# HGRN heads of a hybrid streaming step: triangle work on VectorE, one-bank PSUM tiles, and tail pieces placed next to the level scores

## The chip, the core and the metric

The kernel runs on one core of a Trainium2 chip (trn2). The core has TensorE (PE; its weight loads are listed apart as PEld), VectorE (DVE), ScalarE (ACT), GpSimd (POOL) and the queue of SyncE (SP) that starts DMAs. Each engine works through its own queue in order and waits for others on semaphores. The metric is the device time of one execution in microseconds (us). All times below are of the kernel before.

## The reference

One step of an encoder layer: an mLSTM branch and an HGRN2 branch over the same 544 steps (512 of a new stream, 32 of a running one), merged by sigmoid gates. The change touches the HGRN2 branch alone, 8 heads of width 128:

```python
lfh = jnp.log(lb + (1.0 - lb) * jax.nn.sigmoid(f_lin))
kh = (1.0 - lb) * jax.nn.sigmoid(-f_lin)
qh = jax.nn.silu(q_h)
...
def _hgrn_chunk(S, inp):                    # one 64-step chunk of one head
    q, k, v, lf = inp
    g = jnp.cumsum(lf, axis=2)
    dec = jnp.exp(jnp.where(causal, g[:, :, :, None, :] - g[:, :, None, :, :], -jnp.inf))
    a = jnp.einsum('bhtc,bhtsc,bhsc->bhts', q, dec, k)
    o = jnp.einsum('bhtc,bhce->bhte', q * jnp.exp(g), S) + jnp.einsum('bhts,bhse->bhte', a, v)
    g_last = g[:, :, -1:, :]
    S_new = jnp.exp(g_last[:, :, 0, :])[..., None] * S + jnp.einsum('bhsc,bhse->bhce', k * jnp.exp(g_last - g), v)
    return S_new, o
...
oh = _head_rmsnorm(oh, hnorm_g) * jax.nn.silu(g_h)
yb = oh @ w_brh
y = sigmoid(ga) * ya + sigmoid(gb) * yb
```

The kernel returns the layer's output, the new states of both branches and the last rows of the convolution.

## The kernel before

The kernel is one instruction stream per engine, with 544 steps laid out along the free dimension and 128 channels on the partitions. First come the norm, the input projections and the mLSTM branch (heads 0 to 3, until about 645 us), then the eight HGRN heads (645 to 943 us), then the output projections.

**Projections as background.** Class `Pump` holds a list of projection blocks. A block is 12 or 24 matmuls into the PSUM tiles `d` (line 526), over split weights: ScalarE rounds a weight piece to its high part (`high_piece`, line 133), VectorE subtracts to get the low part (`low_piece`, 138) and forms sums of pieces (484). `pump.to(n)` emits background work up to step n, `pump.run(chain(h))` interleaves it with a generator's work: each `yield k` there lets k steps (12 matmuls each in this stage) pass. So the order of all engines around the change is written out by hand, through `STEPS`, `PIECES`, `TRICKLE` and the `yield`s, and PE, ACT and DVE run exactly this order (`manual_schedule`).

**A head.** `chain(h)` (the two scans are covered by running half of the stream backwards, so that one matmul serves both) builds the score tile `at`: 128 partitions by two blocks of 128 columns, and 32 more for the running stream. Step 0 makes the same-step scores `pd` (lines 1596, 1597; VectorE copies them through the mask `dmask` into `at` and `diag`, 1599, 1600). Then come seven levels c = 1, 2, 4 ... 64. Each needs the keys and queries scaled by the decays of that level: PE makes `pl` (1608, 1616), VectorE multiplies keys and queries for the next level (1625), multiplies neighbouring decays (1630), copies the level's scores into `at` where the level mask allows it (1636), and ScalarE gathers the next level's keys into `km` (1576). The queries of a new head are first multiplied by their decays (line 1469). At the end GpSimd splits `at` into its two triangles `aa` (1646 twice, 1652 for the running stream) and adds `diag` (1653).

**A tail.** `tail(h)` is cut at its `yield`s into pieces that are emitted while the next head's chain runs; `PIECES` says at which point (twice the level, plus one behind its scores; the entry (1, k) is two heads later). The pieces: transposes of values and of keys (`ht`, 1676, 1677; copied out by ScalarE, 1678, 1679), state products `su` (1686, 1687), their accumulation on VectorE (1692, 1702), the output `ho` (1710 to 1714), squares on ScalarE (1725), the inverse root on VectorE (181 to 188, spread by `TRICKLE`), the scaling on ScalarE (1731), and `finish`: transposes `hoT` (1755, 1756) and the gated product (1759, 1760).

**PSUM.** Eight banks of 512 floats. Four hold the `d` tiles. The others are two tiles `paux` of two banks each, used in turn by `pd`, `pl`, `ht`, `su`, `ho`, `hoT`: a new one waits until the last but one is read out. GpSimd zeroes `at`, `kit` and `osb` for each head anew (1569, 1670, 1717).

## Time and profile before

| | |
|---|---|
| median of three runs | 1157.86 us (1157.77 to 1157.99) |
| profiled execution | 1158.48 us, span 1156.8 us |
| granted TensorE clock | 0.998 |
| steady head (state of heads 2 to 6) | 33.79 us from key transposes to key transposes |
| PE, DVE, ACT, POOL busy within it | 32.47, 31.87, 24.38, 4.75 us |

The span lies within the execution's time: 1.7 us are outside of it. The page counts an engine as busy while an instruction is in it; matmul records overlap, so a PE that is listed as busy can still lose time. Losses are better read from the starts of matmuls that follow each other. A row of the timeline gives start, duration, engine, line, operation, output and inputs, and in brackets the idle time before it with what ended it.

### The profile page before, as it was taken

To read this page: it belongs to the slowest core of one execution; us is meant where nothing else is said; L and a number is where in the kernel's file an instruction comes from. 1 tells how busy PE (TensorE), PEld (TensorE's weight loads), DVE (VectorE), ACT (ScalarE), POOL (GpSimd) and SP (SyncE) were. 2 spreads that over 40 slices of the span, in tenths; PEclk is the share of its full clock that TensorE was granted. 3 is DMA by queue.
4 is the path that set the end of the run, shared out by engine and by line. 5 is a ranking of instruction groups with operands and counts; after the bars stand their busy time and mean duration, and the time that the engine had idled before them with its cause. 6 is when DMAs were issued, how large, how long until landed. Compare 5 with 4: busy or idle time off the path is not lost.

```text
span 1156.8 us, 23858 instructions
## 1 busy us (share of the span) xinstructions
PE 1130.9 (98%) x8937; PEld 1113.0 (96%) x8937; DVE 920.1 (80%) x2030; ACT 697.0 (60%) x1517; POOL 147.2 (13%) x306
## 2 busy tenths in 40 slices
PE   9989999999999999999999999999999999999998
PEld 8989999999999999999999999999999999999998
DVE  6876989576896777976887889999999988654585
ACT  5676647655666556664655477777667767433462
POOL 5833000111010110101200011111111100000000
PEclk9999999999999999999999999999999999999999
DMA  6143214322264132552636222212222343234653
GB/s 216 56 136 97 83 56 149 122 87 103 78 212 153 38 138 83 172 194 67 229 107 223 66 81 65 80 54 72 80 69 77 102 159 110 96 114 137 223 194 114
DMA packets 77899, 135.78 MB, mean 117 GB/s; under 512 B 8788, under 2 KB 16340, under 8 KB 77784
## 3 DMA queue, kind: packets, MB, share of 16 engines
q1 hardware_dynamic: 77616, 134.21, 35.7%
q8 instruction: 70, 1.15, 0.4%
q14 instruction: 45, 0.37, 0.1%
q10 hardware_dynamic: 168, 0.06, 0.0%
HBM read 109.32 MB, written 24.91 MB: 116 GB/s over the span
## 4 chain that ended last, share of the span: by engine, by line
PE 77%; DVE 16%; ACT 4%; issue 2%; DMA 2%; SPq 0%; ACTq 0%; DVEq 0%
PE d L526 29%; PE ya L167 8%; PE pg L1829 4%; PE yb L167 4%; PE o L167 4%; PE k L167 4%; PE C L1000 4%; PE q L167 4%; PE nm L1174 2%; PE sc L960 2%; DVE ws L484 2%; DVE hkq L1625 1%; PE pl L1608 1%; PE d L409 1%; DVE cv L723 1%
## 5 line engine op out<-in xcount | busy, mean ns | idle before, releaser
L1576 ACT COPY km<-hkq 128x256 f32<-128x256 f32 x56 | 23.9, 427 | 47.9 <-DVE hkq L1625 30.1
L543 ACT COPY t<-d 128x272 f32<-128x272 f32 x126 | 47.3, 376 | 5.1 <-PE d L526 4.7
L1625 DVE TENSOR_TENSOR hkq<-hkq,hq 128x288 f32<-128x288 f32 (+1 forms) x96 | 41.0, 434 | 6.1 <-PE pl L1616 4.7
L1608 PE MATMUL pl<-hkq,km 128*128 128x128 f32 x224 | 37.9, 291 | 4.1 <-ACT kit L1679 3.3
L723 DVE SCALAR_TENSOR_TENSOR cv<-ub,vec,cv 128x547 f32<-128x547 f32 x48 | 40.3, 841 | 0.6
L1608 PEld LDWEIGHTS pl<-hkq,km 128*128 128x128 f32 x224 | 31.0, 189 | 5.2 <-ACT kit L1679 4.0
L1103 DVE SCALAR_TENSOR_TENSOR c<-c,wi,Cs 128x258 f32<-128x258 f32 x32 | 15.3, 478 | 23.7 <-PE Cs L1101 23.6
L1012 ACT COPY Co<-C 128x258 f32<-128x258 f32 x32 | 10.4, 377 | 30.8 <-PE C L1000 24.0
L1636 DVE COPY_PREDICATED at<-lmask,pl 128x288 f32<-128x288 uint8 (+1 forms) x56 | 26.4, 471 | 0.0
L1646 POOL TENSOR_TENSOR aa<-at,tri 128x256 f32<-128x256 f32 x16 | 17.6, 1126 | 67.2 <-DVE at L1636 67.2
L1242 DVE TENSOR_TENSOR y<-ya,y 128x272 f32<-128x272 f32 x48 | 18.8, 434 | 8.1 <-PE ya L167 7.0
L1185 ACT COPY y<-nm 128x516 f32<-128x516 f32 x16 | 9.5, 591 | 22.6 <-PE nm L1174 22.6
L911 DVE TENSOR_TENSOR kl<-kf,kh 128x512 fp32r<-128x512 f32 x16 | 11.0, 688 | 13.9 <-ACT kh L910 11.9
L1652 POOL TENSOR_TENSOR at<-at,tri 32x32 f32<-32x32 f32 x8 | 4.8, 597 | 135.1 <-DVE at L1636 135.1
L974 ACT CAST sh<-dm 128x512 fp32r<-128x512 f32 (+3 forms) x16 | 7.3, 459 | 20.3 <-DVE dm L968 20.3
L1000 PE MATMUL C<-vh,kwh 128*128 128x258 f32 x96 | 19.4, 283 | 0.0
L1000 PE MATMUL C<-vh,kwl 128*128 128x258 f32 x96 | 19.3, 283 | 0.0
L1000 PE MATMUL C<-vl,kwh 128*128 128x258 f32 x96 | 19.3, 283 | 0.0
L960 PE MATMUL sc<-q,kh 128*128 128x512 f32 (+3 forms) x80 | 18.6, 321 | 0.1
L1133 DVE BATCH_NORM_STATS2 bs<-y 128x6 f32<-128x512 f32 (+1 forms) x20 | 13.8, 689 | 6.1 <-ACT y L1185 5.9
L887 POOL COPY vsm<-vt 128x96 f32<-128x96 f32 x16 | 7.3, 465 | 86.7 <-ACT vt L554 43.7
L1803 DVE TENSOR_TENSOR gb<-yb,gb 128x272 f32<-128x272 f32 x16 | 6.3, 436 | 15.0 <-PE yb L167 15.0
(4528 smaller groups left out, 5095.0 us busy)
## 6 DMA issues: line engine op xcount, KB each, us to landing
ya_d<-y SPq DMA_DIRECT2D x32, 272.0 KB, 3.0
y<-ya_d SPq DMA_DIRECT2D x24, 272.0 KB, 3.3
c<-in_C SPq DMA_DIRECT2D x16, 258.0 KB, 3.7
out_Cp<-Co SPq DMA_DIRECT2D x16, 258.0 KB, 2.6
out_Cs<-c SPq DMA_DIRECT2D x16, 258.0 KB, 2.4
x<-in_xT SPq DMA_DIRECT2D x8, 272.5 KB, 4.7
ya<-ya_d SPq DMA_DIRECT2D x8, 272.0 KB, 4.3
h<-in_xT SPq DMA_DIRECT2D x8, 272.0 KB, 5.0
```

Of the source, the lines that this page charges most:

```text
L167: PE.matmul(both[b][:m, :TH], part(w, off + k * step, m, x), xx[:, half(b)], start=(k == 0 and j == 0), stop=(k == n - 1 and j == 2),)
L484: V.tensor_tensor(q[name], x, y, ALU.add)
L526: PE.matmul(ps, ww[:, c], xx, start=(start and k == 0 and j == 0), stop=end, skip_group_check=not start,)
L543: S.copy(t, ps)
L723: V.scalar_tensor_tensor(cv[:, :547], ub[:, j : j + 547], vcol(V_CW + 4 * ft + j), cv[:, :547], ALU.mult, ALU.add)
L960: PE.matmul(pn[:, 0, :n], ks[f][x][:, j * P : (j + 1) * P], qs[f][y][:, NS + j * P : T], start=(f == 0 and i == 0), stop=(f == KH - 1 and ...
L1000: PE.matmul(pn[g][:, :VH], kw[b][x][:, f * P : (f + 1) * P], vv[b][y][:, g * VH : (g + 1) * VH], start=(b == 0 and j == 0), stop=(b == NB ...
L1576: S.copy(km.rearrange("p (n j c) -> p n j c", j=2, c=c), view(kk, HB, ((2 * c, NA // (2 * c)), (c - HB, 2), (1, c))),)
L1608: PE.matmul(pn[:, 0, b * P : (b + 1) * P], km[:, b * P : (b + 1) * P], view(qq, b * P, ((2 * c, P // (2 * c)), (HB + c, 2), (1, c))), star ...
L1625: V.tensor_tensor(x, x, t, ALU.mult)
L1636: V.copy_predicated(at[:, :n], lmask[:, li, :n], pn[:, 0, :n])
L1829: PE.matmul(ps, part(w, k * P, P, x), xx[:, c], start=(k == 0 and j == 0), stop=(k == KD - 1 and j == 2))
```

## The change

It takes GpSimd out of the HGRN stage. The lower triangle is kept in `at` itself by a multiplication with `down` on VectorE; the other tile `aa` starts as the diagonal of the second `pd` tile (times the identity, on VectorE) and takes the upper triangle of `at` through the mask `up`. Both run seven steps into the next head (`APART`). ScalarE, not VectorE, now copies the first `pd` tile into `at`. `at`, `kit`, `osb` and `hv` become pairs of tiles that are zeroed once (`hv` set to one). The two two-bank tiles become four tiles of one bank, in a pool that exists for this stage only. `PIECES`, `TRICKLE` and the `yield`s move the tail's pieces to stand directly before or behind a level's scores; the query product's delay goes from 2 to 3 steps.

```diff
+APART = 7
+FDELAY = (1, 2, 3)
+QDELAY = 3
...
-PIECES = ((0, 0), (0, 2), (0, 4), (0, 5), (0, 6), (0, 9), (0, 13), (1, 4))
-TRICKLE = (2, 2, 2)
+PIECES = ((0, 1), (0, 4), (0, 6), (0, 6), (0, 7), (0, 8), (0, 13), (1, 5))
+TRICKLE = (1, 1, 2)
...
-    pa = ctx.enter_context(tc.tile_pool(name="pa", bufs=2, space=bass.MemoryType.PSUM))
+    psum = {}
+
+    def aux_pool(name, bufs):
+        if psum:
+            psum["stack"].close()
+        psum["stack"] = ExitStack()
+        psum["a"] = psum["stack"].enter_context(
+            tc.tile_pool(name=name, bufs=bufs, space=bass.MemoryType.PSUM, side="right", reuse_waits="tile")
+        )
+
+    aux_pool("pa", 2)
+    ctx.callback(lambda: psum["stack"].close())
...
-        return pa.tile([P, 2, 512], F32, tag="a", name=name)
+        return psum["a"].tile([P, 2, 512], F32, tag="a", name=name)
+
+    def pone(name):
+        return psum["a"].tile([P, 512], F32, tag="b", name=name)
...
-    tri = cp.tile([P, 2, P], F32, name="tri")
-    pick(tri[:, 0, :], ALU.is_ge, 0, 1, -1, 1.0, 0.0)
-    pick(tri[:, 1, :], ALU.is_gt, 0, -1, 1, 1.0, 0.0)
+    down = cp.tile([P, HB], F32, name="down")
+    for b in range(2):
+        pick(down[:, b * P : (b + 1) * P], ALU.is_ge, 0, 1, -1, 1.0, 0.0)
+    G.memset(down[:, 2 * P :], 0.0)
+    G.tensor_copy(down[:NS, 2 * P :], down[:NS, :NS])
     sxt = cp.tile([P, P], F32, name="sxt")
-    dmask = cp.tile([P, HB], U8, name="dmask")
+    up = cp.tile([P, 2 * P], U8, name="up")
...
-        G.memset(dmask, 0.0)
...
+        pick(sxt, ALU.is_gt, 0, -1, 1, 1.0, 0.0)
+        V.tensor_scalar(
+            up.rearrange("p (b t) -> p b t", b=2),
+            sxt.rearrange("p (o t) -> p o t", o=1).to_broadcast([P, 2, P]),
+            1.0,
+            None,
+            ALU.is_equal,
+        )
...
-            pump.defer(2, lambda: V.tensor_tensor(qq[:, :T], t[:, :T], tf[:, :T], ALU.mult))
+            pump.defer(QDELAY, lambda: V.tensor_tensor(qq[:, :T], t[:, :T], tf[:, :T], ALU.mult))
...
-    diag = small("diag", [P, 2, P], bufs=1, tag="ksm")
-    G.memset(diag, 0.0)
+    aux_pool("pb", 4)
+    ats = [tp.tile([P, NA + P], F32, tag="bc", name=f"at{i}") for i in range(2)]
+    aas = tp.tile([P, 2, 2, P], F32, tag="kws", name="aas", bufs=1)
+    kits = [small(f"kit{i}", [P, 2, P], tag="qw") for i in range(2)]
+    osbs = [small(f"osb{i}", [P, P], tag="osb") for i in range(2)]
+    hvs = [small(f"hv{i}", [P, 5], tag="hv") for i in range(2)]
+    for i in range(2):
+        G.memset(ats[i][:, NA:], 0.0)
+        G.memset(kits[i], 0.0)
+        G.memset(osbs[i], 0.0)
+        G.memset(hvs[i], 1.0)
...
-        at = tp.tile([P, NA + P], F32, tag="bc", name=f"at{h}")
-        G.memset(at, 0.0)
+        at = ats[h % 2]
...
-                yield STEPS[li] // 2
+                yield STEPS[li]
                 advance(h, 0)
-                yield STEPS[li] - STEPS[li] // 2
-                pn = paux(f"pd{h}")
+                pn = pone(f"pd{h}0"), pone(f"pd{h}1")
                 for j in range(2):
                     for b in range(2):
                         x = slice(j * HB + b * P, j * HB + (b + 1) * P)
-                        PE.matmul(pn[:, j, b * P : (b + 1) * P], kk[:, x], q0[:, x], start=True, stop=True)
-                PE.matmul(pn[:, 0, NA:HB], kk[:, wide], q0[:, csmp], start=True, stop=True)
-                with tc.high_priority():
-                    V.copy_predicated(at[:, :HB], dmask, pn[:, 0, :HB])
-                    V.copy_predicated(diag.rearrange("p b t -> p (b t)"), dmask[:, :NA], pn[:, 1, :NA])
+                        PE.matmul(pn[j][:, b * P : (b + 1) * P], kk[:, x], q0[:, x], start=True, stop=True)
+                PE.matmul(pn[0][:, NA:HB], kk[:, wide], q0[:, csmp], start=True, stop=True)
+                S.copy(at[:, :NA], pn[0][:, :NA])
+                S.copy(at[:NS, NA:HB], pn[0][:NS, NA:HB])
+                aa = aas[:, h % 2]
+                V.tensor_tensor(
+                    aa,
+                    pn[1][:, :NA].rearrange("p (b t) -> p b t", b=2),
+                    ident.rearrange("p (o t) -> p o t", o=1).to_broadcast([P, 2, P]),
+                    ALU.mult,
+                )
             else:
-                yield STEPS[li] // 2
+                yield STEPS[li]
                 advance(h, 2 * li)
-                yield STEPS[li] - STEPS[li] // 2
-
-            pn = paux(f"pl{h}{c}")
+
+            pn = pone(f"pl{h}{c}")
             for b in range(2):
                 PE.matmul(
-                    pn[:, 0, b * P : (b + 1) * P],
+                    pn[:, b * P : (b + 1) * P],
                     km[:, b * P : (b + 1) * P],
                     view(qq, b * P, ((2 * c, P // (2 * c)), (HB + c, 2), (1, c))),
                     start=True,
                     stop=True,
                 )
             if smp:
-                PE.matmul(pn[:, 0, NA:HB], kk[:, wide], qq[:, csmp], start=True, stop=True)
+                PE.matmul(pn[:, NA:HB], kk[:, wide], qq[:, csmp], start=True, stop=True)
...
-                V.copy_predicated(at[:, :n], lmask[:, li, :n], pn[:, 0, :n])
+                V.copy_predicated(at[:, :n], lmask[:, li, :n], pn[:, :n])
...
-        aa = tp.tile([P, 2, 2, P], F32, tag="kws", name=f"aa{h}", bufs=1)
-        for j in range(2):
-            G.tensor_tensor(
-                aa[:, j],
-                at[:, :NA].rearrange("p (b t) -> p b t", b=2),
-                tri[:, j : j + 1, :].to_broadcast([P, 2, P]),
-                ALU.mult,
-            )
-        G.tensor_tensor(at[:NS, NA:HB], at[:NS, NA:HB], tri[:NS, 0, :NS], ALU.mult)
-        G.tensor_tensor(aa[:, 1], aa[:, 1], diag, ALU.add)
+        def apart():
+            V.copy_predicated(aa.rearrange("p b t -> p (b t)"), up, at[:, :NA])
+            V.tensor_tensor(at[:, :HB], at[:, :HB], down, ALU.mult)
+
+        pump.defer(APART, apart)
         hs[h].update(at=at, aa=aa, told=told, tsmp=tsmp)
...
-        kit = small("kit", [P, 2, P], tag="qw")
-        kts, its = kit[:, 0], kit[:, 1]
-        G.memset(kit, 0.0)
+        kts, its = kits[h % 2][:, 0], kits[h % 2][:, 1]
+        ps = None
         s0 = small("s0", [P, P], tag="qf")
         nc.sync.dma_start(s0, a["S0"][h])
-        for n, src, dst, dss in ((0, ii, it, its), (1, kk, kt, kts)):
-            pt = paux(f"ht{h}")
+        for src, dst in ((ii, it), (kk, kt)):
+            pt = pone(f"ht{h}")
             for b, (c, _, _) in enumerate(chunks):
-                PE.transpose(pt[:, 0, b * P : (b + 1) * P], src[:, c], ident)
-            PE.transpose(pt[:NS, 1, :P], src[:, csmp], ident)
-            S.copy(dst, pt[:, 0, :])
-            S.copy(dss[:NS], pt[:NS, 1, :P])
+                PE.transpose(pt[:, b * P : (b + 1) * P], src[:, c], ident)
+            if src is ii:
+                ps = pone(f"hs{h}")
+                for n, x in ((1, ii), (0, kk)):
+                    PE.transpose(ps[:NS, n * P : (n + 1) * P], x[:, csmp], ident)
+            S.copy(dst, pt)
+            if src is ii:
+                S.copy(kits[h % 2][:NS], two(ps[:NS, : 2 * P]))
             yield 1
-
-        pu = paux(f"su{h}")
+        pu, pv = pone(f"su{h}"), pone(f"sv{h}")
         for b in range(NB):
             c = slice(b * P, (b + 1) * P)
-            PE.matmul(pu[:, 0, c], kt[:, c], it[:, c], start=True, stop=True)
-        PE.matmul(pu[:, 1, :P], kts, its, start=True, stop=True)
+            PE.matmul(pu[:, c], kt[:, c], it[:, c], start=True, stop=True)
+        PE.matmul(pv[:, :P], kts, its, start=True, stop=True)
         sb = tf
-        S.copy(sb[:, :P], pu[:, 0, :P])
+        S.copy(sb[:, :P], pu[:, :P])
         yield 1
         for b, ti in ((1, 0), (2, 2), (3, 3)):
...
-        po = paux(f"ho{h}")
+        po, pq = pone(f"ho{h}"), pone(f"hp{h}")
         for b, (c, i, j) in enumerate(chunks):
             d = slice(b * P, (b + 1) * P)
-            PE.matmul(po[:, 0, d], aa[:, j, i, :], it[:, d], start=True, stop=(b == 0))
+            PE.matmul(po[:, d], (aa if j else at[:, :NA].rearrange("p (b t) -> p b t", b=2))[:, i, :], it[:, d], start=True, stop=(b == 0))
             if b:
-                PE.matmul(po[:, 0, d], qq[:, c], sb[:, (b - 1) * P : b * P], start=False, stop=True)
-        PE.matmul(po[:, 1, :P], at[:, wide], its, start=True, stop=False)
-        PE.matmul(po[:, 1, :P], qq[:, wide], s0, start=False, stop=True)
+                PE.matmul(po[:, d], qq[:, c], sb[:, (b - 1) * P : b * P], start=False, stop=True)
+        PE.matmul(pq[:, :P], at[:, wide], its, start=True, stop=False)
+        PE.matmul(pq[:, :P], qq[:, wide], s0, start=False, stop=True)
         ov = slot(f"ov{h}")
-        osb = small("osb", [P, P])
-        G.memset(osb, 0.0)
-        S.copy(ov[:, :NP], po[:, 0, :])
-        S.copy(osb[:NS], po[:NS, 1, :P])
-        hv, hr = small("hv", [P, 5]), small("hr", [P, 5])
-        V.memset(hv, 1.0)
+        osb = osbs[h % 2]
+        S.copy(ov[:, :NP], po)
+        S.copy(osb[:NS], pq[:NS, :P])
+        hv, hr = hvs[h % 2], small("hr", [P, 5])
...
+    aux_pool("pc", 2)
```

Places where this moves instructions, taken from head 2's chain (a digit behind a name is the head; `pl24` is head 2, level 4; rows of `d`, weights and the repeats of `ho` are left out at the dots).

PE at the border of two heads, before (`ht1` are head 1's transposes, values then keys):

```order
L1676 MATMUL ht1_10025<-ident_102,hi1_9394 128x128 x4
L1677 MATMUL ht1_10025<-ident_102,hi1_9394 32x128
...
L1596 MATMUL pd2_10061<-hq2_9592,hkq2_9901 128x128 x4
L1597 MATMUL pd2_10061<-hq2_9592,hkq2_9901 128x32
L1608 MATMUL pl21_10069<-hkq2_9901,km21_10000 128x128 x2
L1616 MATMUL pl21_10069<-hkq2_9901 128x32
...
L1676 MATMUL ht1_10100<-ident_102,hkq1_9461 128x128 x4
L1677 MATMUL ht1_10100<-ident_102,hkq1_9461 32x128
```

and in the change:

```order
L1621 MATMUL pd20_10054<-hq2_9594,hkq2_9914 128x128 x2
L1621 MATMUL pd21_10055<-hq2_9594,hkq2_9914 128x128 x2
L1622 MATMUL pd20_10054<-hq2_9594,hkq2_9914 128x32
L1638 MATMUL pl21_10064<-hkq2_9914,km21_10007 128x128 x2
L1646 MATMUL pl21_10064<-hkq2_9914 128x32
L1700 MATMUL ht1_10078<-ident_102,hi1_9415 128x128 x4
L1704 MATMUL hs1_10083<-ident_102,hi1_9415 32x128
L1704 MATMUL hs1_10083<-ident_102,hkq1_9482 32x128
...
L1700 MATMUL ht1_10176<-ident_102,hkq1_9482 128x128 x4
L1638 MATMUL pl24_10182<-hkq2_9914,km24_10137 128x128 x2
```

The value transposes stood 12 projection matmuls ahead of `pd` and the key transposes 12 behind `pl21`; now the first stand right behind `pl21` and the second right before level 4. The first pair of `pd` products and the second are separate tiles.

PE around state products and output, before:

```order
L1686 MATMUL su1_10155<-hi1_9394,hkq1_9461 128x128 x4
L1687 MATMUL su1_10155<-kit_10021 128x128
L1755 MATMUL hoT0_10162<-anti_121,ov0_9777 128x128 x2
L1755 MATMUL hoT0_10162<-ident_102,ov0_9777 128x128 x2
L1756 MATMUL hoT0_10162<-anti_121,osb_9778 128x128
...
L1608 MATMUL pl24_10189<-hkq2_9901,km24_10135 128x128 x2
L1616 MATMUL pl24_10189<-hkq2_9901 128x32
...
L1710 MATMUL ho1_10232<-hi1_9394,aa1_9993 128x128 x2
L1713 MATMUL ho1_10232<-kit_10021,at1_9546 128x128
L1714 MATMUL ho1_10232<-s0_10023,hkq1_9461 128x128
...
L1608 MATMUL pl28_10270<-hkq2_9901,km28_10197 128x128 x2
```

and in the change:

```order
L1713 MATMUL su1_10245<-hi1_9415,hkq1_9482 128x128 x4
L1714 MATMUL sv1_10246<-kit1_8773 128x128
L1638 MATMUL pl28_10260<-hkq2_9914,km28_10190 128x128 x2
L1646 MATMUL pl28_10260<-hkq2_9914 128x32
L1737 MATMUL ho1_10272<-hi1_9415,at1_8770 128x128 x2
...
L1740 MATMUL hp1_10273<-kit1_8773,at1_8770 128x128
L1741 MATMUL hp1_10273<-s0_10076,hkq1_9482 128x128
```

`su` and `ho` of head 1 had `hoT`, 24 projection matmuls and level 4 between them; now only level 8 stands between them.

DVE behind level 4, before:

```order
L1636 COPY_PREDICATED at2_9998<-lmask_2933,pl24_10189 128x288
L1692 SCALAR_TENSOR_TENSOR tf1_9240<-tf1_9240,hq1_9239,su1_10155 128x128 x3
L1702 SCALAR_TENSOR_TENSOR sn_10205<-s0_10023,hq1_9239,su1_10155 128x128
L138 TENSOR_TENSOR ws151l_10208<-ws151_9967,ws151h_10175 128x512
L484 TENSOR_TENSOR ws175_10214<-wi67r0_9965,wi67r1_10037 128x512
L484 TENSOR_TENSOR ws275_10216<-ws175_10214,wi75r0_9963 128x512
L1721 MEMSET hv_10247 128x5
L550 TENSOR_TENSOR hq3_10047<-d511_10046,t151_10073 128x272
L138 TENSOR_TENSOR wa2251l_10252<-wi59r1_9819,wa2251h_10218 128x512
```

and in the change:

```order
L1666 COPY_PREDICATED at0_8769<-lmask_2935,pl24_10182 128x288
L1784 SCALAR_TENSOR_TENSOR ob0_10201<-hoT0_10194,vec_78,hg0_9131 128x512
L1785 SCALAR_TENSOR_TENSOR ob0_10201<-hoS0_10195,vec_78,hg0_9131 128x32
L155 TENSOR_TENSOR ws151l_10204<-ws151_9980,ws151h_10162 128x512
L503 TENSOR_TENSOR ws175_10210<-wi67r0_9978,wi67r1_10031 128x512
L503 TENSOR_TENSOR ws275_10212<-ws175_10210,wi75r0_9976 128x512
L569 TENSOR_TENSOR hq3_10040<-d511_10039,t151_10068 128x272
L155 TENSOR_TENSOR wa2251l_10229<-wi59r1_9831,wa2251h_10214 128x512
L1719 SCALAR_TENSOR_TENSOR tf1_9261<-tf1_9261,hq1_9260,su1_10245 128x128 x3
L1729 SCALAR_TENSOR_TENSOR sn_10257<-s0_10076,hq1_9260,sv1_10246 128x128
```

The state accumulation (1692, now 1719) stood directly behind level 4's copy; now the gated product and five projection instructions are ahead of it.

28 lines of the change are left out of this document (10 added, 18 removed).

## The prediction

> **What bounds the kernel now.** First the page's busy shares:
>
> ```profile
> PE 1130.9 (98%) x8937; PEld 1113.0 (96%) x8937; DVE 920.1 (80%) x2030; ACT 697.0 (60%) x1517; POOL 147.2 (13%) x306
> ```
>
> TensorE is occupied nearly throughout, so the total moves only if TensorE loses less time between matmuls or gets fewer. GpSimd's 147 us bound nothing by themselves. Next the table by stretches, one steady head (from its key transposes to the next head's) and the end of the stage; columns are stretch, length, then busy time and instruction count of PE, PEld, DVE, ACT and POOL, PE clock, DMA share and GB/s:
>
> ```profile
> 779.12:812.91 33.79, 32.47 (x259) 31.72 (x260) 31.87 (x83) 24.38 (x59) 4.75 (x7) 1.00 0.20 69
> 880.48:943.00 62.52, 62.48 (x507) 62.02 (x508) 58.40 (x140) 42.94 (x110) 4.06 (x5) 1.00 0.36 112
> ```
>
> The clock is full, DMA is light. VectorE has 1.9 us of slack in the 33.79 us of a head, so it can fall behind TensorE but hardly catch up; ScalarE has over 9. Third, TensorE's waits within the HGRN stage (us in total, times, longest):
>
> ```profile
> PE pl L1608 <- ACT kit L1679: 3.3, 6, 0.6
> PE pd L1596 <- DVE at L1636: 2.6, 6, 0.5
> PE ht L1676 <- DVE diag L1600: 1.7, 6, 0.3
> ```
>
> Each occurs six times, at the borders of heads 2 to 7, and each is for a PSUM tile of the ring of two to be read out. The listed lengths are too short, since matmul records overlap. So, fourth, one such border in TensorE's timeline, read by starts:
>
> ```profile
> 710.99 0.29 PE L526 MATMUL d<-xfh,ws174l 128*128 128x272 f32 x1
> 711.56 0.63 PE L1676 MATMUL ht<-ident,hkq 128*128 128x128 f32 x4 [0.29 <-DVE diag L1600]
> ...
> 712.05 0.38 PE L526 MATMUL d<-xfh,wa2274h 128*128 128x272 f32 x1
> 712.26 0.29 PE L526 MATMUL d<-xfl,wa2274h 128*128 128x272 f32 x1
> 712.39 0.29 PE L526 MATMUL d<-xfh,wa2274l 128*128 128x272 f32 x1
> ...
> 713.66 0.64 PE L1608 MATMUL pl<-hkq,km 128*128 128x128 f32 x4
> ...
> 714.28 0.37 PE L526 MATMUL d<-xfh,ws251h 128*128 128x272 f32 x1
> ...
> 721.11 0.28 PE L526 MATMUL d<-xh,wa1251l 128*128 128x272 f32 x1
> 721.44 0.68 PE L1710 MATMUL ho<-hi,aa 128*128 128x128 f32 x4
> ...
> 739.89 0.29 PE L526 MATMUL d<-xh,wa1152l 128*128 128x272 f32 x1
> 740.60 1.13 PE L1596 MATMUL pd<-hq,hkq 128*128 128x128 f32 x8 [0.42 <-DVE at L1636]
> 741.57 0.31 PE L1597 MATMUL pd<-hq,hkq 128*128 128x32 f32 x2
> 742.43 0.92 PE L1608 MATMUL pl<-hkq,km 128*128 128x128 f32 x4 [0.55 <-ACT kit L1679]
> ...
> 743.33 0.37 PE L526 MATMUL d<-xfh,ws175h 128*128 128x272 f32 x1
> ```
>
> Ordinary `d` matmuls start 0.13 us apart (712.26 to 712.39). Against that spacing TensorE loses 740.60 - 740.02 = 0.58 us before `pd`; after `pd` (whose 32-column end takes about 0.1 from 741.57) some 0.72 before `pl`; 0.28 in `pl` itself, which takes 0.90 to the next `d` where an unhindered one takes 714.28 - 713.66 = 0.62; 711.56 - 711.12 = 0.44 before the key transposes; and 721.44 - 721.24 = 0.20 before `ho`. That is 2.22 us per head. Without them a head takes 31.57 us.
>
> **What makes VectorE late at the border.** Fifth, GpSimd and VectorE there:
>
> ```profile
> 740.60 2.20 POOL L1646 TENSOR_TENSOR aa<-at,tri 128x256 f32<-128x256 f32 x2 [8.54 <-DVE at L1636]
> 742.88 1.06 POOL L1653 TENSOR_TENSOR aa<-aa,diag 128x256 f32<-128x256 f32 x1
> ```
>
> ```profile
> 740.35 0.68 DVE L138 TENSOR_TENSOR wa2275l<-wi67r,wa2275h 128x512 fp32r<-128x512 f32 x1
> 740.95 1.27 DVE L1469 TENSOR_TENSOR hkq<-hq,tf 128x544 f32<-128x544 f32 x1
> 742.14 1.21 DVE L138 TENSOR_TENSOR ws252l<-ws,ws252h 128x512 fp32r<-128x512 f32 x1
> 743.28 1.22 DVE L484 TENSOR_TENSOR ws<-ws,wi52r 128x512 f32<-128x512 f32 x1
> 744.42 0.47 DVE L1599 COPY_PREDICATED at<-dmask,pd 128x288 f32<-128x288 uint8 x1
> 744.78 0.43 DVE L1600 COPY_PREDICATED diag<-dmask,pd 128x256 f32<-128x256 uint8 x1
> ```
>
> While GpSimd works on `aa` (740.60 to 743.94), three VectorE instructions that read two SBUF tiles are long: 1.27, 1.21 and 1.22 us; the one ahead, of the same shape as the second and third, takes 0.68. For the 544-column one the whole kernel shows both lengths (count, then min/median/max ns):
>
> ```profile
> L1469 DVE TENSOR_TENSOR hkq<-hq,tf x8: 712/1266/1272, 619.3 to 876.1; 128x544 f32<-128x544 f32 x8
> ```
>
> So the loss is 0.56 + 0.53 + 0.54 = 1.63 us per head, and it falls just where the new head's query product (line 1469, needed by `pl`), and the `pd` copies (needed to free the tile for the key transposes) are waited for.
>
> [...]
>
> **The change, part by part.**
>
> *GpSimd removed.* VectorE gains 1.63 us per head. The zeroings it also did delayed nobody on the path; they vanish at no gain.
>
> *VectorE's added work.* Two instructions of 256 columns (identity times `pd`; masked copy of the upper triangle), each like the 0.43 of row 744.78, and a product of 288 columns, half of the pair at 729.99 below, 0.46: +1.32. Removed: the two copies at 744.42 and 744.78, 0.90, and a tiny memset. Net VectorE gain 1.2 us per head: 31.87 to about 30.7. All three lie inside VectorE's queue; the triangle pair stands ahead of the level-2 scaling, where VectorE is at its tightest, but `ho` wants its result some three levels later.
>
> *ScalarE's added work.* A copy of 256 and one of 32 columns, less one of the two `kit` copies. Prices, from the page's groups (busy, mean ns) and a timeline:
>
> ```profile
> L543 ACT COPY t<-d 128x272 f32<-128x272 f32 x126 | 47.3, 376 | 5.1 <-PE d L526 4.7
> ```
>
> ```profile
> 740.12 0.51 ACT L1576 COPY km<-hkq 128x256 f32<-128x256 f32 x1
> 740.54 0.62 ACT L133 CAST ws252h<-ws 128x512 fp32r<-128x512 f32 x1
> ...
> 742.12 0.25 ACT L1679 COPY kit<-ht 32x128 f32<-32x128 f32 x1
> ```
>
> At most 0.38 + 0.25, less 0.25: +0.4 us on 24.4, hidden in ScalarE's waits for VectorE. But its place counts: the tile for the 32-row transposes (`hs`) is the fifth of a ring of four, so it waits until ScalarE has emptied `pd`. ScalarE was busy without a break from 740.12 to the end of `kit` at 742.37. Now the copies end after one more weight cast (0.5) and one `d` copy (0.3), less the `ht` and `kit` copies (0.7) and plus 0.6 of their own: about 743.1. With `pl` ending near 742.4 and the value transposes 0.5 behind it, `hs` comes at 742.9: a wait of 0 to 0.3. I take 0, because `pl` is held by something later, next.
>
> *PSUM ring of four.* `pd` now takes a tile that was emptied a level or more before: 0.58 goes. The key transposes move to level 4: 0.44 goes. What is late next is `pl`, through the query product in VectorE's queue. From the scaling after level 16 to that product VectorE runs without a pause:
>
> ```profile
> 728.76 0.61 PE L1608 MATMUL pl<-hkq,km 128*128 128x128 f32 x4
> ```
>
> ```profile
> 729.99 0.91 DVE L1625 TENSOR_TENSOR hkq<-hkq,hq 128x288 f32<-128x288 f32 x2
> ```
>
> that is 740.95 - 729.99 = 10.96 us, and the same instructions stand there afterwards. TensorE's way from the end of level 16 (728.76 + 0.62 = 729.38) to `pd` was 10.64 without the 0.58; the value transposes leave it (0.49, row 711.56 to 712.05 for the same size, and a re-entry of 0.08, below), and `pd` adds 1.1: 11.2 to `pl`. VectorE needs 0.1 to start, 10.96, 0.71 for the product and 0.1 to signal: 11.9. So `pl` waits 0.7 if VectorE meets level 16 on time, and 1.2 if it is as late there as now (729.99 - 729.38 = 0.6). I take 0.7, because VectorE has 1.2 us less to do. The 0.28 inside `pl` and 0.2 before `ho` I leave. Residue 1.2 (bounds 0 and 1.7) of the 2.22.
>
> *Pieces next to scores.* The first `d` after a piece takes 0.21 (712.05 to 712.26), not 0.13: 0.08 each. By the order, a head has 11 such returns before and 7 now: 4 x 0.08 = 0.3 us saved. The 32-row transposes are the same work.
>
> *Outside the heads.* The masks made at the start and the later `up` cost GpSimd about as much as `tri` and `dmask` did. VectorE's mask instruction waits for GpSimd's selection on `sxt`; a weight subtraction and a convolution step stand between, and if that cover fails it is one wait of about a microsecond. On SP the state's output DMA now goes behind one more weight load: earlier loads, no one waits. `QDELAY` moves nothing on VectorE. All counted as 0.
>
> *Sum.* Per head 2.22 - 1.2 + 0.3 = 1.3 us (bounds 2.5 and 0.8). Six borders: 7.8. The border of heads 0 and 1, where ScalarE rather than GpSimd is late, and the last head's tail: 1 together (0.3 to 2). Total 9 us (bounds 5 and 17). The profiled execution of 1158.5 becomes 1149.5; it stood 0.6 above the median, so the time is **1149 us** (1141 to 1153).
>
> **The rivals.**
>
> *Slower: VectorE's state sums.* `su` and `ho` had 24 projection matmuls between them; now only level 8 (0.62) does. The sums between them were at:
>
> ```profile
> 717.71 0.75 DVE L1759 SCALAR_TENSOR_TENSOR ob<-hoT,vec,hg 128x512 f32<-128x512 f32 x1 [0.67 <-PE hoT L1756]
> ...
> 719.84 0.92 DVE L1625 TENSOR_TENSOR hkq<-hkq,hq 128x288 f32<-128x288 f32 x2 [0.18 <-PE pl L1616]
> ...
> 721.19 1.10 DVE L1692 SCALAR_TENSOR_TENSOR tf<-tf,hq,su 128x128 f32<-128x128 f32 x3
> ...
> 722.46 0.68 DVE L138 TENSOR_TENSOR ws151l<-ws,ws151h 128x512 fp32r<-128x512 f32 x1
> ...
> 724.75 0.68 DVE L138 TENSOR_TENSOR wa2251l<-wi59r,wa2251h 128x512 fp32r<-128x512 f32 x1
> ```
>
> They came directly behind level 4. Now `ob` (0.75, and a small one) and the stretch from 722.46 to 725.35 (2.9) stand ahead, 3.7 us. From the end of level 4 VectorE needs 1.35 (719.84 to 721.19), 3.7 and 0.35 for the first sum, 5.4. TensorE reaches the `ho` that reads it after `hoT` (0.5), 24 projections (3.1), `su` (1.1), level 8 (0.6) and about 0.9 of `ho`: 6.2. So 0.8 us of slack decides. At the border VectorE reaches the `pd` copy 2.7 us after `pd` (744.42 against 741.7); were it 3.5 late at level 4, TensorE would lose 2.7 in each of seven heads, 19 us against the 9 saved: 1168. Against it: row 719.84 finds VectorE waiting for `pl`, so the lateness is worked off by then, and the 1.6 us are gone. Chance 0.10.
>
> *The waits change places.* `hs` waits for ScalarE (0.3 to 1 us), `pl` the full 1.2, `ho` a little: 0.3 to 0.8 us saved per head, 1153 to 1157. For it: ScalarE does not pause from 740.12 to 742.37, and the copies stand at the end of a longer run. Chance 0.16.
>
> *It doesn't do what it says.* The long instructions could come from something other than GpSimd, ScalarE's copies for instance. Then VectorE gets 0.4 us more per head, `pl` waits about 2 and the ring and the returns save some 0.5: 1155. Against it: the row with 0.71 and 1.27 for one form, and GpSimd's times beside it. Chance 0.04.
>
> *All of it goes.* If VectorE stays ahead, `pl` does not wait: 17 us, 1141. Chance 0.05.
>
> **How the numbers follow.** The forecast, 1141 to 1153, has the remaining 0.65. The range is 1141 to 1156: below the upper end lie the forecast and most of the second and third rival. A difference under 0.2%, 2.3 us, cannot be told from none. Faster: the forecast, the last rival and most of the second and third, 0.84; no change, 0.06; slower, 0.10.
>
> **What would show it.** The 544-column product must be 0.71 us in all heads and the two behind it about 0.68; GpSimd idle from 645 us. TensorE's waits for `at` before `pd` and for `diag` must be gone; `pl` at a border should wait for VectorE's query product, about 0.7. Steady heads should take 32.3 to 32.6 us. `ho` must not wait on line 1719, nor `hs` on line 1623; if either does by more than a microsecond per head, the forecast is wrong.

## The result: 1157.92 us before, 1149.84 us after

Medians of four executions each: 1157.92 us (1157.77 to 1158.10) before, 1149.84 us (1148.69 to 1151.14) after; ratio 0.993, 95% interval 0.9913 to 0.9948. Forecast: 1149, with 1141 to 1156 as the range. The profiled execution of the changed kernel took 1151.14 us, its span is 1148.7.

The page's busy shares of the changed kernel, then one steady head in the table by stretches (stretch, length, busy time and count of PE, PEld, DVE, ACT, POOL, PE clock, DMA share, GB/s):

```profile
PE 1127.3 (98%) x8937; PEld 1114.4 (97%) x8937; DVE 910.1 (79%) x2029; ACT 699.5 (61%) x1525; POOL 111.4 (10%) x260
```

```profile
773.67:805.98 32.31, 31.65 (x262) 31.54 (x261) 30.75 (x83) 24.55 (x61) 0.00 (x0) 1.00 0.24 76
```

A head now takes 32.31 us from key transposes to key transposes, against 33.79. VectorE has 30.75 us of work in it (31.87 before), ScalarE 24.55 (24.38), GpSimd none. TensorE's waits from 640 to 975 us of the changed kernel:

```profile
PE pl L1638 <- DVE hkq L1487: 4.6, 7, 0.7
```

Of the three waits of the kernel before, those ahead of `pd` and of the transposes are gone, and the one ahead of `pl` has changed its releaser. One border in TensorE's timeline of the changed kernel:

```profile
738.42 0.29 PE L545 MATMUL d<-xh,wa1152l 128*128 128x272 f32 x1
738.55 1.11 PE L1621 MATMUL pd<-hq,hkq 128*128 128x128 f32 x8
739.49 0.31 PE L1622 MATMUL pd<-hq,hkq 128*128 128x32 f32 x2
740.46 0.89 PE L1638 MATMUL pl<-hkq,km 128*128 128x128 f32 x4 [0.66 <-DVE hkq L1487]
741.18 0.31 PE L1646 MATMUL pl<-hkq 128*128 128x32 f32 x2
741.33 0.64 PE L1700 MATMUL ht<-ident,hi 128*128 128x128 f32 x4
741.80 0.27 PE L1704 MATMUL hs<-ident,hi 128*32 128x128 f32 x1
```

`pd` follows `d` at the ordinary 0.13 us, `ht` and `hs` follow without a gap. By starts, `pl` comes 0.97 us behind the end part of `pd`, which needs 0.14 where nothing waits (646.85 to 646.99 in the first head), so 0.83 us are lost. On VectorE, what held it is the product of 739.59, behind a weight subtraction:

```profile
738.63 0.45 DVE L1666 COPY_PREDICATED at<-lmask,pl 128x256 f32<-128x256 uint8 x1
738.98 0.69 DVE L155 TENSOR_TENSOR wa2275l<-wi67r,wa2275h 128x512 fp32r<-128x512 f32 x1
739.59 0.72 DVE L1487 TENSOR_TENSOR hkq<-hq,tf 128x544 f32<-128x544 f32 x1
740.23 0.69 DVE L155 TENSOR_TENSOR ws252l<-ws,ws252h 128x512 fp32r<-128x512 f32 x1
740.83 0.68 DVE L503 TENSOR_TENSOR ws<-ws,wi52r 128x512 f32<-128x512 f32 x1
741.43 0.42 DVE L1626 TENSOR_TENSOR aas<-pd,ident 128x256 f32<-128x256 f32 x1
```

The instructions that took 1.27, 1.21 and 1.22 us take 0.72, 0.69 and 0.68. From the first `pd` to the first matmul of the stage that follows, the HGRN heads take 325.7 us (645.96 to 971.70) where they took 335.1 (645.03 to 980.14): 9.4 us less. The span became 8.1 us shorter; the rest was lost outside the heads, which comes at the end.

### The profile page after: what moved, and what is told of

It is laid out like the page before. It is cut to its first block, busy times and chain, and to the rows that moved or that the text cites. A ratio compares the mean times of both kernels' runs of the same rounds, so it can differ in the third digit from the quotient of the medians.

```text
span 1148.7 us, 23733 instructions
## 1 busy us (share of the span) xinstructions
PE 1127.3 (98%) x8937; PEld 1114.4 (97%) x8937; DVE 910.1 (79%) x2029; ACT 699.5 (61%) x1525; POOL 111.4 (10%) x260
## 4 chain that ended last, share of the span: by engine, by line
PE 80%; DVE 13%; ACT 3%; DMA 2%; issue 2%; SPq 0%; ACTq 0%; DVEq 0%
PE d L545 31%; PE ya L184 8%; PE yb L184 4%; PE pg L1855 4%; PE o L184 4%; PE k L184 4%; PE C L1019 4%; PE q L184 4%; PE nm L1193 2%; PE sc L979 2%; PE pl L1638 2%; PE d L428 2%; DVE hkq L1655 1%; DVE cv L742 1%; DVE ws L503 1%
## 5 line engine op out<-in xcount | busy, mean ns | idle before, releaser
L1842 DVE TENSOR_TENSOR h<-o,h 128x272 f32<-128x272 f32 x16 | 6.3, 436 | 15.0 <-PE o L184 13.2
L1193 PE MATMUL nm<-vh,sh 128*128 128x258 f32 x80 | 16.4, 287 | 0.1
L1193 PE MATMUL nm<-vl,sh 128*128 128x258 f32 x80 | 16.2, 284 | 0.0
```

The costliest lines, as they stand in the source:

```text
L1193: PE.matmul(pn[:, g, :VH], st[j][x][:, (i - j) * P : (i - j + 1) * P], vv[j][y][:, g * VH : (g + 1) * VH], start=(j == 0 and q == 0), stop ...
```

## The experiments

Twelve kernels were run, each beside the kernel before on the same chip. "Head" is the median interval between the starts of `pd` in the steady heads, read from TensorE's timeline of one profiled execution; outside a dip of the clock it repeats within 0.1 us from head to head (one head of e5, 0.35 us longer, excepted), and so tells more than the whole time, whose executions scatter by 1.3 us (e12) to 6 us (e5).

| Kernel | median us (range, executions) | before, same chip | ratio, 95% interval | head us |
|---|---|---|---|---|
| before | 1157.92 (1157.77 to 1158.10, 4) | | | 33.79 |
| changed | 1149.84 (1148.69 to 1151.14, 4) | 1157.92 | 0.993, 0.9913 to 0.9948 | 32.32 |
| e1 GpSimd load | 1150.36 (1149.71 to 1153.08, 6) | 1158.53 | 0.993, 0.9917 to 0.9943 | 32.31 |
| e2 two tiles of two banks | 1168.91 (1168.19 to 1169.58, 4) | 1158.53 | 1.0085, 1.0072 to 1.0098 | 34.77 |
| e3 old places | 1153.75 (1152.01 to 1154.22, 5) | 1158.53 | 0.995, 0.9938 to 0.9963 | 32.78 |
| e4 GpSimd's part alone | 1160.35 (1159.28 to 1163.00, 11) | 1158.53 | 1.0015, 1.0006 to 1.0024 | 33.82 |
| e5 GpSimd kept | 1163.76 (1161.90 to 1167.85, 6) | 1158.67 | 1.0041, 1.0026 to 1.0057 | 34.13 |
| e6 e4, old transposes | 1158.94 (1156.51 to 1160.76, 12) | 1158.67 | 1.000, 0.9991 to 1.0008 | 33.68 |
| e7 e3, old transposes | 1152.04 (1150.94 to 1152.52, 5) | 1158.67 | 0.9936, 0.9924 to 0.9948 | 32.88 |
| e8 product first | 1148.21 (1147.03 to 1150.24, 4) | 1158.67 | 0.9905, 0.9891 to 0.9919 | 32.19 |
| e9 GpSimd on the product | 1152.68 (1151.94 to 1155.37, 5) | 1158.36 | 0.9953, 0.9941 to 0.9965 | 32.58 |
| e10 sums later | 1153.21 (1152.54 to 1156.09, 6) | 1158.36 | 0.9956, 0.9944 to 0.9968 | 33.03 |
| e11 `hs` in `pd` | 1149.73 (1148.88 to 1151.08, 4) | 1158.36 | 0.9924, 0.9911 to 0.9937 | 32.40 |
| e12 with fillers | 1149.67 (1148.99 to 1150.27, 4) | 1158.36 | 0.9922, 0.9909 to 0.9935 | 32.40 |

### Is it GpSimd? (e1, e9)

```diff
+        G.tensor_copy(sxt[:, 0:2], at[:, 0:2])
+        for _ in range(6):
+            G.tensor_tensor(sxt, down[:, :P], ident, ALU.mult)
         pump.defer(APART, apart)
```

> The changed kernel, with GpSimd given six products of 128x128 (two SBUF inputs, result into a tile nobody reads) at the end of each head, where it made the triangles before; nothing else differs. Theory A (contention with GpSimd was the 1.63 us per head): the query product (line 1487) grows from 0.72 to about 1.25 us and the two or three VectorE instructions behind it grow too; TensorE's wait before `pl` grows from 0.66 to about 1.2 us; a steady head takes 32.9 to 33.9 us, the whole 1154 to 1160. Rival (the long instructions came from something else, which the change also removed): line 1487 stays at 0.72, the whole stays at 1149 to 1151.

Nothing moved: a head takes 32.31 us. GpSimd and VectorE at one border of this kernel:

```profile
737.36 0.51 POOL L1678 COPY sxt<-at 128x2 f32<-128x2 f32 x1 [27.23 <-DVE at L1666]
737.94 4.48 POOL L1680 TENSOR_TENSOR sxt<-down,ident 128x128 f32<-128x128 f32 x6
```

```profile
737.74 0.72 DVE L1487 TENSOR_TENSOR hkq<-hq,tf 128x544 f32<-128x544 f32 x1
738.37 0.94 DVE L155 TENSOR_TENSOR ws252l<-ws,ws252h 128x512 fp32r<-128x512 f32 x1
739.24 0.94 DVE L503 TENSOR_TENSOR ws<-ws,wi52r 128x512 f32<-128x512 f32 x1
```

The product had started 0.2 us ahead of the load and kept its 0.72; the two behind it grew to 0.94. So GpSimd does lengthen them, as theory A has it, but time lost behind the product costs TensorE nothing. e9 leaves the copy out, so that the load begins earlier, its first product reading `at`:

```diff
+        for j in range(6):
+            G.tensor_tensor(sxt, (down if j else at)[:, :P], ident, ALU.mult)
         pump.defer(APART, apart)
```

> The changed kernel with the same GpSimd load as in the first run (six products of 128x128 per head), begun some 0.6 us earlier, so that the query product runs under it. In the first run such a load lengthened a VectorE instruction with two SBUF inputs by 0.26 us (0.68 to 0.94), and nothing was lost because the product had already started. Theory A (contention costs time only through the query product, which `pl` waits for): the product takes about 0.98 us, the wait before `pl` grows from 0.66 to 0.9 us or a little more, a steady head from 32.32 to 32.6 (up to 32.8 if the subtraction ahead is hit as well), the whole about 1152. Rival (a load on GpSimd takes no time from TensorE here at all): 32.32 and 1150.

```profile
771.02 0.69 DVE L155 TENSOR_TENSOR wa2276l<-wi68r,wa2276h 128x512 fp32r<-128x512 f32 x1
771.63 0.98 DVE L1487 TENSOR_TENSOR hkq<-hq,tf 128x544 f32<-128x544 f32 x1
772.53 0.94 DVE L155 TENSOR_TENSOR ws253l<-ws,ws253h 128x512 fp32r<-128x512 f32 x1
```

The product grew by 0.26 us and the head by 0.26 (32.58): theory A, to the hundredth. Contention is real, and its price is what it adds to this one instruction.

### One part alone, and each part undone (e2 to e7)

e2 undoes the ring: two tiles of two banks, everything else as changed. What is shown for `pd` is done for the other pairs (`ht` and `hs`, `su` and `sv`, `ho` and `hp`, `hoT` and `hoS`) and for `pl`, which uses the first bank.

```diff
-    aux_pool("pb", 4)
+    aux_pool("pb", 2)
-                pn = pone(f"pd{h}0"), pone(f"pd{h}1")
+                pn = pone2(f"pd{h}")
+    def pone2(name):
+        t = paux(name)
+        return t[:, 0], t[:, 1]
```

> The changed kernel with its four one-bank PSUM tiles put back into two of two banks; GpSimd idle, pieces at the new places. Theory A (ring and places belong together): `ho` now needs the tile that `su` used, and the state sums leave that 1.3 us later than `ho` is reached; the key and value transposes need the tile of `pd`, read out 0.5 us too late; 1.5 to 2 us per head, so 1160 to 1165, slower than the kernel before. Rival (the ring is worth only the wait before `pd` and that before the transposes, and GpSimd the rest): 1152 to 1155.

TensorE's waits in this kernel's heads:

```profile
PE ho L1737 <- DVE sn L1729: 8.6, 7, 1.2
PE pl L1639 <- DVE hkq L1488: 4.6, 7, 0.7
PE ht L1701 <- DVE aas L1627: 4.2, 7, 0.6
```

The two waits that theory A named, 1.2 and 0.6 us, came, and the head lost more than that, 2.45 us: by starts they cost 1.40 and 0.79, and `hoT` comes 0.23 late as well. The whole, 1168.91, lies above the 1165 expected. The new places cannot be had without the ring.

e3 puts the places back, e4 places and ring, which leaves GpSimd's part (idle GpSimd, triangles on VectorE, `pd` read out by ScalarE). The step is split in the same way at the first level.

```diff
-PIECES = ((0, 1), (0, 4), (0, 6), (0, 6), (0, 7), (0, 8), (0, 13), (1, 5))
-TRICKLE = (1, 1, 2)
+PIECES = ((0, 0), (0, 2), (0, 4), (0, 5), (0, 6), (0, 9), (0, 13), (1, 4))
+TRICKLE = (2, 2, 2)
-                yield STEPS[li]
-                advance(h, 2 * li)
+                yield STEPS[li] // 2
+                advance(h, 2 * li)
+                yield STEPS[li] - STEPS[li] // 2
```

> The changed kernel with the head-tail's pieces back at the old places, in the middle of the steps (old PIECES, TRICKLE and split steps); ring of four and idle GpSimd stay. Theory A (places are worth the cheaper returns to `d`, 4 per head at 0.08): about 0.3 us per head, 1151 to 1153. Rival (the places also set when buffers come free or who is late, so they are worth a us per head or more): 1156 or more. A second rival: the old places are better, since they leave the state sums more time: 1147 or less.

> Only the first part of the change: triangles on VectorE and tiles zeroed once, with two two-bank PSUM tiles and the old places. Theory A (VectorE's 1.2 us per head pays even in the old ring): the wait before `pd` (0.58) goes and the one before the key transposes shrinks, the one before `pl` stays on ScalarE's copy; about 1 us per head, 1150 to 1153. Rival (without the ring the waits are for the tiles themselves and hardly move): 1155 to 1158.

Both were spoiled by something I had overlooked. The waits of e3:

```profile
PE hs L1706 <- DVE hkq L1657: 6.9, 7, 1.5
```

The changed tail makes both 32-row transposes in its first piece. At the old place that piece stands ahead of the new head's `pd`, where the old head's keys have not had their last scaling; e4 has the same wait. So both were run again with the transposes as in the kernel before, one behind each piece (`ps` is the second bank of the piece's tile in e6, a tile of its own in e7):

```diff
-            if src is ii:
-                ps = pone(f"hs{h}")
-                for n, x in ((1, ii), (0, kk)):
-                    PE.transpose(ps[:NS, n * P : (n + 1) * P], x[:, csmp], ident)
+            PE.transpose(ps[:NS, :P], src[:, csmp], ident)
```

> GpSimd's part alone once more: two two-bank PSUM tiles, old places, and now also the old order of the 32-row transposes (one behind each of the two pieces). The run with GpSimd's part alone that moved both 32-row transposes into the first piece took 1160.35, and TensorE waited there up to 1.5 us for the last scaling of the keys (line 1658). Theory A (that wait was the only thing that spoiled it, 6.9 us in all): 1152 to 1155. Rival (idle GpSimd is worth nothing in the old ring): 1157 to 1160.

> The changed kernel with the old places and the old order of the 32-row transposes; ring of four and idle GpSimd stay. With the old places alone it took 1153.75, 6.9 us of it waiting at `hs` for the keys' last scaling. Theory A (the wait at `hs` goes and nothing takes its place; what remains are 4 cheaper returns per head): 1147 to 1150, no worse than the changed kernel, so that the new places are worth nothing by themselves. Rival (the wait at `pl` for the query product, which `hs` had hidden, comes back with 4 to 5 us): 1151 to 1154.

e6, GpSimd's part alone, is worth nothing on balance: 1158.94 beside 1158.67, 0.11 us per head. Of the three waits of the kernel before, those ahead of `pl` and `pd` stay, the one ahead of the key transposes is gone, and one ahead of `hoT` is new:

```profile
PE pl L1641 <- ACT kit L1706: 4.1, 7, 0.6
PE pd L1623 <- DVE at L1669: 2.3, 6, 0.4
PE hoT L1779 <- DVE at L1669: 1.1, 6, 0.2
```

By starts the key transposes no longer lose their 0.44 us (they follow the `d` ahead of them by 0.13 instead of 0.57), and the stretch from `su` to `hoT` takes 0.36 longer (1.47 instead of 1.11): `hoT` needs a tile that VectorE reads out only behind its two new triangle instructions (0.86 us), which stand ahead of the level-2 scaling. So this part does free TensorE of one wait right behind the border, and the work that replaces GpSimd's costs nearly as much in the ring of two.

VectorE did get its 1.63 us back, 1.2 net of the added work, and spent most of that waiting. In its timeline of e6 one head has these waits:

```profile
775.67 0.42 DVE L1628 TENSOR_TENSOR aas<-pd,ident 128x256 f32<-128x256 f32 x1 [1.30 <-ACT at L1626]
...
782.96 0.75 DVE L1783 SCALAR_TENSOR_TENSOR ob<-hoT,vec,hg 128x512 f32<-128x512 f32 x1 [0.35 <-PE hoT L1780]
...
785.07 0.92 DVE L1658 TENSOR_TENSOR hkq<-hkq,hq 128x288 f32<-128x288 f32 x2 [0.18 <-PE pl L1649]
...
791.09 0.92 DVE L1658 TENSOR_TENSOR hkq<-hkq,hq 128x288 f32<-128x288 f32 x2 [0.43 <-PE pl L1649]
```

The kernel before has the last three of them too (0.66, 0.18 and 0.43), 1.27 us in all where e6 has 2.26. So the time that GpSimd took from VectorE behind one border had been made up some 10 us later, long before the next border, and giving it back moved nothing there: `pd` and `pl` lose 0.54 and 0.76 us by starts, where they lost 0.58 and 0.72. The 1.30 us is for ScalarE's copies out of the same two-bank tile; with one-bank tiles (e7) VectorE does not wait there.

e7 adds the ring: 1152.04, 0.80 us per head better than e6. The wait that remains, ahead of `pl`, is for ScalarE's copy of the value transposes (`hi`, 5.7 us in seven times). Theory A had expected no wait; the rival had the size, 4 to 5 us, but not the releaser. From e7 to the changed kernel, places and transposes together are worth 0.56 us per head.

e5 asks the reverse: ring and places as changed, GpSimd's part as before, with its zeroings and with `pd` read out by the two masked copies on VectorE.

```diff
-        pump.defer(APART, apart)
+        for j in range(2):
+            G.tensor_tensor(
+                aa[:, j],
+                at[:, :NA].rearrange("p (b t) -> p b t", b=2),
+                tri[:, j : j + 1, :].to_broadcast([P, 2, P]),
+                ALU.mult,
+            )
+        G.tensor_tensor(at[:NS, NA:HB], at[:NS, NA:HB], tri[:NS, 0, :NS], ALU.mult)
+        G.tensor_tensor(aa[:, 1], aa[:, 1], diag, ALU.add)
```

> The changed kernel's ring of four and its places, with the triangles, zeroings and masked `pd` copies of the kernel before, so that GpSimd works on `aa` at each border again. The first run of this series put a GpSimd load there, but it began after the query product had started, and the time did not move. Theory A (what costs time is that GpSimd hits the query product, which `pl` waits for): the product takes 1.2 to 1.3 us, TensorE waits 1.1 to 1.3 us before `pl` instead of 0.66, 0.5 us per head, 1153 to 1156. Theory B (VectorE as a whole is late by the 1.63 us and TensorE loses it all at the next levels): 1158 to 1162. Rival (GpSimd costs nothing once the ring and the places are new): 1149 to 1151.

At 1163.76 it is slower than the kernel before. One border, TensorE and then VectorE:

```profile
778.00 0.89 PE L1624 MATMUL pl<-hkq,km 128*128 128x128 f32 x4 [1.20 <-ACT ws476h L150]
...
780.59 0.28 PE L1697 MATMUL hs<-ident,hi 128*32 128x128 f32 x1 [1.08 <-DVE at L1616]
```

```profile
776.60 1.26 DVE L1486 TENSOR_TENSOR hkq<-hq,tf 128x544 f32<-128x544 f32 x1
777.78 1.23 DVE L155 TENSOR_TENSOR ws253l<-ws,ws253h 128x512 fp32r<-128x512 f32 x1
778.93 1.21 DVE L501 TENSOR_TENSOR ws<-ws,wi53r 128x512 f32<-128x512 f32 x1
780.07 0.46 DVE L1616 COPY_PREDICATED at<-dmask,pd 128x288 f32<-128x288 uint8 x1
```

The product ends at 777.86, 0.14 us ahead of `pl`, so that is what `pl` waits for, whatever the row names. That costs 0.54 us more than in the changed kernel, as theory A had it; the other 1.08 is `hs`, which needs a `pd` tile that VectorE empties behind three long instructions. The sum, 1.62, is most of the 1.81 us per head between the two kernels; by starts the two come to 0.53 and 1.24, 1.77. Theory B had about the size (1.63 us per head; the time lies above its 1162) and not the place.

These runs also show what sets how late VectorE is at level 16, from where it runs without a pause to the query product. Level 16 and VectorE's scaling behind it, in e5 with GpSimd at work, and in e6 with GpSimd idle:

```profile
799.05 0.61 PE L1624 MATMUL pl<-hkq,km 128*128 128x128 f32 x4
799.84 0.92 DVE L1641 TENSOR_TENSOR hkq<-hkq,hq 128x288 f32<-128x288 f32 x2
```

```profile
793.99 0.61 PE L1641 MATMUL pl<-hkq,km 128*128 128x128 f32 x4
795.22 0.92 DVE L1658 TENSOR_TENSOR hkq<-hkq,hq 128x288 f32<-128x288 f32 x2
```

In e5 the scaling starts 0.18 us behind the end of level 16, in e6 0.62. It is 0.6 in the steady heads of every kernel with the old places (the kernel before, e3, e4, e6, e7) and 0.2 in every one with the new places (the changed kernel, e1, e2, e5, e8 to e11), whatever GpSimd does and whichever the ring. So it is the places that bring VectorE there on time.

### What comes after (e8, e11), and the slack of the state sums (e10)

e8 moves the query product one place ahead in VectorE's queue:

```diff
-                self.hook()
+                self.settle(self.done - 0.5), self.hook()
-            pump.defer(QDELAY, lambda: V.tensor_tensor(qq[:, :T], t[:, :T], tf[:, :T], ALU.mult))
+            pump.defer(QDELAY - 1.5, lambda: V.tensor_tensor(qq[:, :T], t[:, :T], tf[:, :T], ALU.mult))
```

> The changed kernel with one pair of VectorE instructions swapped at each border: the query product (line 1487) goes ahead of the weight subtraction that stands before it (0.61 us by starts); nothing else differs on any engine. Theory A (the residue of the forecast: `pl` waits 0.66 us for that product, seven times 4.6 us in all, and nothing else is as late): the wait goes, a steady head takes 31.7 us, the whole 1145 to 1147. Rival (another operand, the keys' copy or the emptying of the `pd` tiles, is as late): 1149 to 1151, with a wait of about the same length on another releaser.

The wait for the product went, and another took most of its place:

```profile
770.11 0.89 PE L1638 MATMUL pl<-hkq,km 128*128 128x128 f32 x4
770.83 0.31 PE L1646 MATMUL pl<-hkq 128*128 128x32 f32 x2
770.98 0.64 PE L1700 MATMUL ht<-ident,hi 128*128 128x128 f32 x4
771.95 0.28 PE L1704 MATMUL hs<-ident,hi 128*32 128x128 f32 x1 [0.34 <-ACT at L1624]
```

By starts `pl` came 0.64 us earlier, and `hs` lost 0.50 of that to ScalarE's copies out of `pd`: 0.13 us per head was left. At 1148.21 it is the fastest of all kernels here, though over the changed one the gain is read from the heads (0.13 each), since the intervals of the two ratios overlap. e11 puts the 32-row transposes into the unused half of the second `pd` tile, to spare `hs` that wait (`spare` holds `pn[1][:, 2 * P :]`):

```diff
-                ps = pone(f"hs{h}")
+                ps = spare.pop() if spare else pone(f"hs{h}")
```

> The kernel with the query product first (1148.21), where TensorE then waited 0.34 us per head at `hs`, for ScalarE's copies out of `pd`; now the 32-row transposes go into the free half of the second `pd` tile, so that `hs` needs no tile of its own. Theory A (that wait is the next and last one at the border): it goes, a steady head takes 31.85 instead of 32.19 us, the whole 1145.5 to 1146.5. Rival (the time moves on to another wait once more, at the level after it or at `ht`): 32.1 to 32.2, 1148.

```profile
PE pd L1705 <- DVE aas L1627: 3.8, 7, 0.6
```

Now the transposes wait for VectorE to read out the other half of that tile; 32.40 us, 0.2 worse than e8. Theory A fell, and the rival's time was not reached either.

e10 delays the state sums by four small products:

```diff
+        for _ in range(4):
+            V.tensor_tensor(sxt, down[:, :P], ident, ALU.mult)
         for b, ti in ((1, 0), (2, 2), (3, 3)):
```

> The changed kernel with four small VectorE products (128x128, about 0.25 us each, 1.0 us together, result into a tile nobody reads) put ahead of the three state sums in each head's tail. The prediction gave those sums 0.8 us of slack before `ho`; the trace of the changed kernel has the first sum end about 0.25 us before the `ho` that reads it. Theory A (0.8): `ho` waits 0.2 us, +1.5 us in all. Theory B (0.25): `ho` waits 0.7 to 0.8 us in each of seven heads, 5 us in all, 1155. Rival (VectorE, with 1.5 us of slack per head, falls behind everywhere and the wait before `pl` grows as well): 1158 or more.

```profile
721.58 1.26 DVE L1719 TENSOR_TENSOR sxt<-down,ident 128x128 f32<-128x128 f32 x4
722.76 1.11 DVE L1721 SCALAR_TENSOR_TENSOR tf<-tf,hq,su 128x128 f32<-128x128 f32 x3
```

```profile
722.18 0.39 PE L1741 MATMUL ho<-tf,hkq 128*128 128x128 f32 x2
722.41 0.39 PE L1739 MATMUL ho<-hi,aas 128*128 128x128 f32 x2
723.15 0.49 PE L1741 MATMUL ho<-tf,hkq 128*128 128x128 f32 x2 [0.36 <-DVE tf L1721]
```

The sums come 1.18 us later, and the second `ho` on `tf` 0.52 us: it starts at 723.15, where the spacing of the rows ahead (0.45 from one such pair to the next) gives 722.63. So the slack was 1.18 - 0.52 = 0.66 us. My theory B of 0.25 was a misreading: the first `ho` on `tf` reads what ScalarE copied, and only the second needs the first sum. The head grew by 0.71 us, and all of it lies within `ho`: from its first row to the next `d` it takes 2.73 us (721.66 to 724.39) instead of 2.01 (755.15 to 757.16 in the changed kernel), since two more pairs behind the wait start 0.33 apart instead of 0.22. The wait ahead of `pl` stayed at 4.6 us.

## Why the prediction was right, step by step

- **The sum.** Forecast: 1.3 us per head, 7.8 at six borders, 1 for the first border and the tail, together 9. Measured: 1.47 in a steady head, 8.8 from the first `pd` to the last (645.03 to 875.72 is 230.7 before, 645.96 to 867.84 is 221.9 now), 0.6 behind the last `pd`; 9.4 in all. Counted from `pd` to `pd`, the six intervals that end at heads 2 to 7 gave 8.35 for the 7.8, and the rest 1.07 for the 1.
- **What leaves.** The 0.58 before `pd` and the 0.44 before the key transposes are gone, as forecast. The 0.20 before `ho`, which the forecast left standing, is gone too. Of the returns to `d`, 11 before, 7 are left, each 0.21 us where 0.13 is usual: 0.3 us, as forecast.
- **What stays.** Forecast 0.7 before `pl` for the query product; the row has 0.66, the starts 0.83. The 0.28 inside `pl` stays: 740.46 to 741.18 is 0.72, in e8 also 0.72 with no wait ahead of it. It is no wait for an operand, then, and what it is stays open. Residue 1.1 where 1.2 was forecast; 2.22 - 1.1 + 0.3 gives 1.4 of the 1.47 measured. The 0.1 for VectorE's start and the 0.1 for its signal had no row in the forecast; the changed kernel shows 0.18 from the end of level 16 to the scaling (760.88 to 761.06) and 0.15 from the end of the product to `pl` (740.31 to 740.46).
- **`hs`.** Taken as 0, bounds 0 to 0.3: no wait in the changed kernel, because `pl` is held by something later, as said. With that removed (e8) it appeared with 0.34. The rival in which waits change places was the right description of the next step.
- **VectorE and ScalarE.** Forecast 30.7 and 24.8 us per head; measured 30.75 and 24.55.
- **The state sums.** Slack forecast 0.8, measured 0.66 (e10); the slower rival missed by that much.
- **Wrong: "GpSimd removed. VectorE gains 1.63 us per head", read as what makes VectorE late at the border.** The contention and its three long instructions are right (e1, e9). But GpSimd's part alone is worth 0.11 us per head (e6): it removes the 0.44 before the key transposes, brings 0.36 before `hoT`, and leaves the waits before `pd` and `pl` as they were. I used the waiting VectorE of row 719.84 against the slower rival, that lateness is worked off before it matters, and did not turn it on my own term. The waits at the next border have other sources: the tile two steps back in the ring, and a VectorE queue that runs without a pause from level 16 on. The choice of 0.7 rather than 1.2 before `pl` fails with it in its reason, "because VectorE has 1.2 us less to do": with GpSimd at work VectorE is just as punctual at level 16 (0.18 in e5), and with GpSimd idle but the old places as late as before (0.62 in e6). The new places did it, which the forecast credited with cheaper returns alone, so the 0.7 came out right by luck. The total escaped the error because it was summed from TensorE's losses and not from VectorE's gain.
- **The three parts are not additive.** In the order GpSimd, ring, places they are worth 0.11, 0.80 and 0.56 us per head; with ring and places there first, they cost 0.34 (e5) and GpSimd's part brings 1.81. That part also moves the reading of the first `pd` tile from VectorE to ScalarE; how the 1.81 divides between this and the contention was not tried apart.
- **Outside the heads, counted as 0:** the first `pd` came 0.9 us later than in the profile before. The dip of the clock shown in the last section costs 1.4 us just ahead of it, more than the whole difference.

## What to carry to other kernels

Time taken from an engine costs only where the next instruction that someone waits for stands behind it: look for the first wait of that engine after the loss, and if there is one before the next critical point, giving the time back is worth nothing. When several edits make one change, undo each alone and try each alone, for here one part alone was worth nothing on balance and two of them without it made the kernel slower. When a wait is removed, the next one is often within half a microsecond (0.66 for `pl`, then 0.34 at `hs`), so count what is left by starts and not by the row that is on top.
